# A row maximum in 22 loads, with parts of the late rows reduced over partitions by GpSimd

## The chip, the cores and the metric

The kernel runs on one core of a Trainium2 chip. The metric is the device time of one execution in microseconds, as the median of repeated runs. One further execution was recorded by the hardware profiler; every duration below comes from that record.

## The reference

The input `x` has the shape 32 x 512 x 1024 in float32. The output is the maximum over the last axis, 32 x 512 values:

```python
def reference(x):
    return np.max(x, axis=-1).astype(np.float32)
```

The first two axes are flattened, so there are 16,384 vectors of 1,024 values. In the kernel 128 of them lie across the 128 partitions. In this document a **row** is such a set: 128 partitions x 1,024 values, 512 KB. The whole input is 128 rows, and one output value per partition comes from each.

## The kernel before

`ring` is a buffer in SBUF with room for `RING = 45` rows. `BLOCKS` lists by hand how many rows each load brings: first 14, 13, 12 and so on, at the end single rows. The loop issues each load from SyncE's queue (line 57) into the next free stretch of the ring and, right after it, VectorE's `reduce_max` over the same stretch (line 58), which writes one column of `res` for each row. VectorE takes the loads in that order. A load into a stretch that VectorE has not yet reduced waits for it; the framework puts in these waits.

The last row comes in two halves of 512 values. The first goes to the ring (line 67) and the second to `tail` (line 68), whose element just ahead of the second half receives the maximum of the first (line 69), so that one reduce over 513 values gives the row's result (line 70). All loads use one queue; SyncE does nothing else. TensorE, ScalarE's compute and GpSimd are unused, but for four small constants that GpSimd writes at the start.

The output goes out in two stores from ScalarE's queue: the first block of 112 rows (line 73), which is held by hand behind the last reduce of the loop, and the second block of 16 rows at the very end (line 75).

Of the kernel before, what the change touches and what calls it, by code (L numbers as in the profile page):

```python
# [1 line left out]

# [4 lines left out]

F32 = mybir.dt.float32

BLOCKS = [
    [14, 13, 12, 11, 9, 8, 8, 7, 6, 5, 5, 4, 4, 3, 3],
    [2, 2, 2, 1, 1, 1, 1, 1, 1, 1, 1, 1],
]
RING = 45
SYNC = mybir.DependencyInfo(mybir.DependencyClass.Sync, mybir.DependencyReason.DATA)

@with_exitstack
def kernel(
    ctx: ExitStack,
    tc: tile.TileContext,
    x: bass.AP,
    out: bass.AP,
):
    nc = tc.nc
    P = 128
    X = mybir.AxisListType.X  # L30

    xf = x.flatten_outer_dims()
    N, D = xf.shape
    H = D // 2
    I = N // P
    of = out.flatten_outer_dims()

    once = ctx.enter_context(tc.tile_pool(name="once", bufs=1))
    ring = once.tile([P, RING, D], F32)
    res = once.tile([P, I], F32)  # L40

    PAD = 16
    tail = once.tile([P, PAD + H], F32)

    at = first = 0
    views = []
    for loads in BLOCKS:
        S = sum(loads) + (loads is BLOCKS[-1])
        xb = xf[first * P:(first + S) * P, :].rearrange("(p i) d -> p i d", p=P)
        dst = bass.AP(tensor=of.tensor, offset=of.offset + first * P, ap=[[S, P], [1, S]])  # L50
        views.append((dst, res[:, first:first + S]))
        b = 0
        for n in loads:
            if at + n > RING:
                at = 0
            xc = ring[:, at:at + n, :]
            nc.sync.dma_start(out=xc, in_=xb[:, b:b + n, :])  # L57
            reduce = nc.vector.reduce_max(out=res[:, first + b:first + b + n], in_=xc, axis=X)  # L58
            at += n
            b += n  # L60
        first += S
    assert first == I

    if at + 1 > RING:
        at = 0
    half = ring[:, at, :H]
    nc.sync.dma_start(out=half, in_=xb[:, b, :H])
    nc.sync.dma_start(out=tail[:, PAD:], in_=xb[:, b, H:])
    nc.vector.reduce_max(out=tail[:, PAD - 1:PAD], in_=half, axis=X)  # L69
    nc.vector.reduce_max(out=res[:, I - 1:], in_=tail[:, PAD - 1:], axis=X)  # L70

    store = nc.scalar.dma_start(out=views[0][0], in_=views[0][1])
    tc.add_manual_dep(store.ins, reduce.ins.name, SYNC, reason="behind the loads")
    nc.scalar.dma_start(out=views[1][0], in_=views[1][1])

# [1 line left out]
_INS = ['x']  # L79
_OUTS = [((32, 512), 'float32')]  # L80

# [23 lines left out]
```

## Time and profile before

| What | Value |
|---|---|
| Median of 10 runs | 164.97 us (164.91 to 165.22) |
| The profiled execution | 164.91 us, of which its span is 163.1 us |
| VectorE busy | 138.9 us, 29 reduces |
| VectorE idle before its reduces | 21.8 us, 20.1 of it before the first |
| Data moved | 67.11 MB of loads, in 29 loads; mean 412 GB/s over the span |
| First load (14 rows) reduced from | 20.13 us |
| Last reduce starts, lasts | 160.12 us, 0.69 us |

The span is the time from the first to the last instruction on the core; the other 1.8 us of the execution's own time lie around it. The share of the DMA engines in the table by slices can pass 1, since packets overlap a little. A wait is put down to the event that came last.

### The profile page before, as it was taken

Reading aid. Unit: us, or ns where it says so; the run is one execution under the profiler, and the core shown is the slowest. Engines: PE = TensorE matmul, PEld = TensorE weight load, DVE = VectorE, ACT = ScalarE, POOL = GpSimd, SP = SyncE. Lnnn points to the kernel's source line nnn. Section 1 sums busy time; section 2 is a strip of 40 time slices with the busy share of each in tenths; the row PEclk is TensorE's granted clock in tenths of the full one; section 3 lists DMA queues with packets and bytes.
Section 4 is the critical chain, followed back from the end, with each engine's and each line's share of the span. In section 5 each row is a group of like instructions: output and inputs, shape, how many; then the busy total and the mean of one; then the engine's idle time right before and its main releaser. Section 6 shows DMA issues by size and latency. Waiting matters only on the chain.

```text
span 163.1 us, 117 instructions
## 1 busy us (share of the span) xinstructions
DVE 138.9 (85%) x29; POOL 0.2 (0%) x4
## 2 busy tenths in 40 slices
DVE  0000099989998999999999999999999999999994
POOL 0000000000000000000000000000000000000000
DMA  6999999999989989999989999999999999999990
GB/s 225 450 450 450 434 418 418 418 402 554 410 386 420 464 387 433 434 434 434 466 386 450 434 450 410 410 445 412 432 423 434 422 422 420 424 411 409 411 369 16
DMA packets 4464, 67.18 MB, mean 412 GB/s; under 512 B 752, under 2 KB 752, under 8 KB 2160
## 3 DMA queue, kind: packets, MB, share of 16 engines
q1 hardware_dynamic: 4176, 67.11, 96.8%
q10 hardware_dynamic: 288, 0.07, 0.2%
HBM read 67.11 MB, written 0.07 MB: 412 GB/s over the span
## 4 chain that ended last, share of the span: by engine, by line
DVE 49%; DMA 48%; SPq 1%; issue 0%
DMA ring<-in_x_dram 48%; DVE res L58 48%; SPq L57 1%; DVE res L70 0%; DVE tail L69 0%
## 5 line engine op out<-in xcount | busy, mean ns | idle before, releaser
L58 DVE TENSOR_REDUCE res<-ring 128x1 f32<-128x1024 f32 (+12 forms) x27 | 137.6, 5162 | 21.8 <-DMA ring<-in_x_dram 21.8
L70 DVE TENSOR_REDUCE res<-tail 128x1 f32<-128x513 f32 x1 | 0.7, 687 | 0.0
L69 DVE TENSOR_REDUCE tail<-ring 128x1 f32<-128x512 f32 x1 | 0.7, 676 | 0.0
L90 POOL MEMSET const-bfloat16-1.0<- 128x1 bf16 x1 | 0.1, 103 | 0.0
L90 POOL MEMSET const-uint8-127<- 128x1 uint8 x1 | 0.1, 103 | 0.0
L90 POOL MEMSET const-float32-1.0<- 128x1 f32 x1 | 0.1, 100 | 0.0
L90 POOL MEMSET const-float32-0.0<- 128x1 f32 x1 | 0.1, 99 | 0.2 <-issue 0.2
## 6 DMA issues: line engine op xcount, KB each, us to landing
ring<-in_x_dram SPq DMA_DIRECT2D x2, 4096.0 KB, 25.6
ring<-in_x_dram SPq DMA_DIRECT2D x1, 7168.0 KB, 19.4
ring<-in_x_dram SPq DMA_DIRECT2D x1, 6656.0 KB, 34.7
ring<-in_x_dram SPq DMA_DIRECT2D x1, 6144.0 KB, 48.7
ring<-in_x_dram SPq DMA_DIRECT2D x1, 5632.0 KB, 28.4
ring<-in_x_dram SPq DMA_DIRECT2D x2, 2560.0 KB, 38.3
ring<-in_x_dram SPq DMA_DIRECT2D x1, 4608.0 KB, 24.7
ring<-in_x_dram SPq DMA_DIRECT2D x9, 512.0 KB, 13.8
```

The source lines that it names most:

```text
L57: nc.sync.dma_start(out=xc, in_=xb[:, b:b + n, :])
L58: reduce = nc.vector.reduce_max(out=res[:, first + b:first + b + n], in_=xc, axis=X)
L69: nc.vector.reduce_max(out=tail[:, PAD - 1:PAD], in_=half, axis=X)
L70: nc.vector.reduce_max(out=res[:, I - 1:], in_=tail[:, PAD - 1:], axis=X)
L90: nc = _bacc.Bacc("TRN2", target_bir_lowering=False, num_devices=1)
```

## The change

In the sequence of loads, `BLOCKS` becomes 18 loads with 126 rows, of 15, 15, 15, 8, 12, 11, 9, 8, 7, 7, 5 and 4, 3, 2, 2, 1, 1, 1 rows, numbered from 0; the last two rows come in halves, four more loads. The ring has 46 rows. SyncE's queue still issues all of them, now at line 181 (and 201 and 202 for the halves).

From six of the late loads a part of the last rows is taken from VectorE. `SHARED` names it: `9: (5, 2)` means that of load 9 the last 5 rows have their first 2 parts of 128 values each handled elsewhere. For such a part `turn` (line 131 on) has TensorE transpose each 128 x 128 piece into PSUM, ScalarE copy the result to SBUF (line 137), and GpSimd take its maximum over the partitions with `partition_all_reduce` (line 139), up to 1,024 columns in one instruction. `back` then has TensorE transpose row 0 of that result, 128 values at a time, into single columns of a small PSUM tile (line 157). VectorE reduces the rest of those rows into one more column of the same small tile (the second `maximum` in the loop), and later `merge` reduces over the columns of the tile into `res`. A load with more than 1,024 columns to turn is taken in two chunks, which is the case for load 9 alone: 1,024 and 256 columns.

The lists fix the order on each engine. `TENSOR` is the order of `turn` and `back`; `MERGE` says after which load's reduces which tile is merged; `in_turn` chains the instructions of an engine in the order in which the program records them. An item of `TENSOR` is recorded as soon as the loads that it needs have been issued in the program, and no more than three loads are issued ahead of the loop's position. Eight small VectorE instructions at the start build the identity matrix for the transposes.

```diff
--- before.py
+++ after.py
 BLOCKS = [
-    [14, 13, 12, 11, 9, 8, 8, 7, 6, 5, 5, 4, 4, 3, 3],
-    [2, 2, 2, 1, 1, 1, 1, 1, 1, 1, 1, 1],
+    [15, 15, 15, 8, 12, 11, 9, 8, 7, 7, 5],
+    [4, 3, 2, 2, 1, 1, 1],
 ]
-RING = 45
+RING = 46
+
+
+SHARED = {9: (5, 2), 11: (4, 2), 12: (2, 4), 14: (1, 2), 15: (1, 4), 17: (1, 2)}
+
+
+TENSOR = [
+    ("turn", 9, 0), ("turn", 9, 1), ("back", 9, 0), ("back", 9, 1),
+    ("turn", 11, 0), ("turn", 12, 0), ("back", 11, 0), ("turn", 14, 0),
+    ("turn", 15, 0), ("back", 12, 0), ("back", 14, 0), ("turn", 17, 0),
+    ("back", 15, 0), ("back", 17, 0),
+]
+
+MERGE = {10: (9,), 13: (11,), 16: (12,), 17: (14,), 20: (15, 17)}
...
     once = ctx.enter_context(tc.tile_pool(name="once", bufs=1))
+    turned = ctx.enter_context(tc.tile_pool(name="turned", bufs=2))
+    allr = ctx.enter_context(tc.tile_pool(name="allr", bufs=2))
+    psum = ctx.enter_context(tc.tile_pool(name="psum", bufs=2, space=bass.MemoryType.PSUM))
+    psmall = ctx.enter_context(tc.tile_pool(name="psmall", bufs=4, space=bass.MemoryType.PSUM))
     ring = once.tile([P, RING, D], F32)
     res = once.tile([P, I], F32)
 
     PAD = 16
-    tail = once.tile([P, PAD + H], F32)
-
-    at = first = 0
+    tails = once.tile([P, 2, PAD + H], F32)
+
+    latest = {}
+
+    def in_turn(engine, inst):
+
+        if engine in latest:
+            tc.add_manual_dep(inst.ins, latest[engine].ins.name, NOSYNC, reason="in turn")
+        latest[engine] = inst
+        return inst
+
...
+
+    ident = once.tile([P, P], F32)
+    colno = once.tile([P, P], F32)
+    rowno = once.tile([P, 32], F32)
+    in_turn("DVE", nc.vector.memset(ident, 1.0))
...
+    loads = []
+    first = at = 0
     views = []
-    for loads in BLOCKS:
-        S = sum(loads) + (loads is BLOCKS[-1])
+    for sizes in BLOCKS:
+        S = sum(sizes) + 2 * (sizes is BLOCKS[-1])
         xb = xf[first * P:(first + S) * P, :].rearrange("(p i) d -> p i d", p=P)
         dst = bass.AP(tensor=of.tensor, offset=of.offset + first * P, ap=[[S, P], [1, S]])
         views.append((dst, res[:, first:first + S]))
         b = 0
-        for n in loads:
+        for n in sizes:
             if at + n > RING:
                 at = 0
-            xc = ring[:, at:at + n, :]
-            nc.sync.dma_start(out=xc, in_=xb[:, b:b + n, :])
-            reduce = nc.vector.reduce_max(out=res[:, first + b:first + b + n], in_=xc, axis=X)
+            loads.append((at, n, xb[:, b:b + n, :], first + b))
             at += n
             b += n
         first += S
     assert first == I
 
-    if at + 1 > RING:
-        at = 0
-    half = ring[:, at, :H]
-    nc.sync.dma_start(out=half, in_=xb[:, b, :H])
-    nc.sync.dma_start(out=tail[:, PAD:], in_=xb[:, b, H:])
-    nc.vector.reduce_max(out=tail[:, PAD - 1:PAD], in_=half, axis=X)
-    nc.vector.reduce_max(out=res[:, I - 1:], in_=tail[:, PAD - 1:], axis=X)
+    def chunks(j):
+        m, parts = SHARED[j]
+        per = max(1, C // parts)
+        return [(r, min(per, m - r)) for r in range(0, m, per)]
+
+    def rows(j):
+        start, n, _, _ = loads[j]
+        return ring[:, start:start + n, :]
+
+    tops = {}
+    backs = {}
+
+    def turn(j, c):
+
+
+        m, parts = SHARED[j]
+        r, q = chunks(j)[c]
+        W = q * parts * P
+        ps = psum.tile([P, D], F32)
+        for i in range(q):
+            for c0 in range(parts):
+                k = i * parts + c0
+                in_turn("PE", nc.tensor.transpose(
+                    out=ps[:, k * P:(k + 1) * P],
+                    in_=rows(j)[:, loads[j][1] - m + r + i, c0 * P:(c0 + 1) * P],
+                    identity=ident,
+                ))
+        sb = turned.tile([P, D], F32)
+        in_turn("ACT", nc.scalar.copy(out=sb[:, :W], in_=ps[:, :W]))
+        top = allr.tile([P, D], F32)
+        in_turn("POOL", nc.gpsimd.partition_all_reduce(
+            top[:, :W], sb[:, :W], P, bass_isa.ReduceOp.max))
+        tops[j, c] = top
+
+    def share(j):
+        m, parts = SHARED[j]
+        if j not in backs:
+            fetched = psmall.tile([P, m, parts + (parts < C)], F32)
+            backs[j] = fetched
+        return backs[j]
+
+    def back(j, c):
+
+        m, parts = SHARED[j]
+        r, q = chunks(j)[c]
+        for i in range(q):
+            for c0 in range(parts):
+                k = i * parts + c0
+                in_turn("PE", nc.tensor.transpose(
+                    out=share(j)[:, r + i, c0:c0 + 1],
+                    in_=tops[j, c][0:1, k * P:(k + 1) * P],
+                    identity=ident[0:1, 0:1],
+                ))
+
+    def maximum(out, in_):
+        return in_turn("DVE", nc.vector.reduce_max(out=out, in_=in_, axis=X))
+
+    def merge(j):
+        for i in MERGE.get(j, ()):
+            _, k, _, c0 = loads[i]
+            q, _ = SHARED[i]
+            maximum(res[:, c0 + k - q:c0 + k], share(i))
+
+
+    issued = done = 0
+    todo = list(TENSOR)
+    for j in range(len(loads)):
+        while issued < len(loads) and issued < j + 3:
+            start, n, src, _ = loads[issued]
+            held = any(s < start + n and start < s + k for s, k, _, _ in loads[j:issued])
+            if held:
+                break
+            nc.sync.dma_start(out=rows(issued), in_=src)
+            issued += 1
+        while todo and (todo[0][0] == "back" or todo[0][1] < issued):
+            what, i, c = todo.pop(0)
+            (turn if what == "turn" else back)(i, c)
+        _, n, _, col = loads[j]
+        m, parts = SHARED.get(j, (0, 0))
+        if n > m:
+            maximum(res[:, col:col + n - m], rows(j)[:, :n - m, :])
+        if m and parts < C:
+            maximum(share(j)[:, :, parts], rows(j)[:, n - m:, parts * P:])
+        merge(j)
+    assert not todo
+
+    for t in range(2):
+        if at + 1 > RING:
+            at = 0
+        row = S - 2 + t
+        half = ring[:, at, :H]
+        at += 1
+        nc.sync.dma_start(out=half, in_=xb[:, row, :H])
+        nc.sync.dma_start(out=tails[:, t, PAD:], in_=xb[:, row, H:])
+        maximum(tails[:, t, PAD - 1:PAD], half)
+        merge(len(loads) + 2 * t)
+        last = maximum(res[:, I - 2 + t:I - 1 + t], tails[:, t, PAD - 1:])
+        merge(len(loads) + 2 * t + 1)
+        if t == 0:
+            latest_row = last
 
 
     store = nc.scalar.dma_start(out=views[0][0], in_=views[0][1])
-    tc.add_manual_dep(store.ins, reduce.ins.name, SYNC, reason="behind the loads")
```

In the list of instructions of the changed program, the order on VectorE from load 9 on is: 2 rows of load 9; the 5 x 768 part of load 9; 5 rows of load 10; merge of 9; the 4 x 768 part of load 11; 1 row and the 2 x 512 part of load 12; 2 rows of load 13; merge of 11; 1 row and the 1 x 768 part of load 14; the 1 x 512 part of load 15; load 16; merge of 12; the 1 x 768 part of load 17; merge of 14; the two halves of the one row; the first half of the other; merges of 15 and 17; the second half.

That list also has the waits that the framework put in. VectorE's reduces of the parts of loads 9, 11, 14, 15 and 17, which write into the small PSUM tile, each wait for TensorE's last `back` into the same tile. For load 12 it is the other way round: TensorE's `back` waits for VectorE's reduce.

## Prediction before the run

> **What bounds the kernel now.** The table of busy time first, then the chain that ended last, then the DMA issues.
>
> ```profile
> DVE 138.9 (85%) x29; POOL 0.2 (0%) x4
> DMA  6999999999989989999989999999999999999990
> ```
>
> VectorE (DVE) works 85% of the span. The second line, the DMA engines' busy share in 40 slices, is full from the second slice to the last but one: two resources are near their limit, and the end decides which one holds it.
>
> ```profile
> 1.62 48.73 DMA ring<-in_x_dram
> ...
> 63.72 30.29 DMA ring<-in_x_dram
> 94.01 0.02 issue
> 94.04 65.45 DVE res L58 x21
> 159.49 0.61 DVE tail L69
> 160.12 0.69 DVE res L70
> ```
>
> The columns are start, duration, what. Up to 94 us the transfers release VectorE each time; from there VectorE runs 65.45 us without a gap and sets the end. Those 21 reduces are 60 rows. A row costs 1.0667 us (the 14-row reduce takes 15,085 ns, the 13-row one 14,020; in between lie the starts of consecutive single rows, 1.126 us apart), so 60 x 1.0667 = 64.0, and 1.45 / 21 = 0.07 us is left for each instruction.
>
> ```profile
> ring<-in_x_dram SPq DMA_DIRECT2D x1, 256.0 KB, 9.6
> tail<-in_x_dram SPq DMA_DIRECT2D x1, 256.0 KB, 9.0
> 149.28 0.33 SPq L67 DMA_DIRECT2D ring<-in_x_dram  x1
> 150.52 0.33 SPq L68 DMA_DIRECT2D tail<-in_x_dram  x1
> ```
>
> The last half was issued at 150.52 and landed 9.0 us later, at 159.5. The reduce that needs it began at 160.12. So VectorE holds the end by only 0.6 us; behind it the transfers would. **That is all that a lighter VectorE can win at this end.** The arrival rate comes from VectorE's first waits, which a load ends: 14 rows at 20.13, 27 at 35.83, 39 at 50.37, thus 1.21 us a row.
>
> [...] VectorE's part and TensorE's `back` write different columns of one small tile and are ordered all the same. The trace before uses no PSUM and can't show it. [...]
>
> **The change, part by part.**
>
> *Loads.* Seven fewer. In the trace's packet records a packet of 57,344 B takes 2,116 ns and one of 4,096 B 162 ns: 27.2 B/ns and some 11 ns for each packet. Each engine carries eight packets of a load, so a load costs about 0.09 us, seven 0.6: the last landing moves from 159.5 to 158.9. Worth nothing, since VectorE ends later. Still, 15 rows first instead of 14 delay VectorE's start to 21.4, and loads 1 and 2 land 18.1 us apart where a 15-row reduce takes 16.1: idle 2.0 us twice. VectorE leaves load 2 at 21.4 + 3 x 16.07 + 4.0 = 73.7; loads 3 to 8, 55 rows, take 58.7 + 0.4, so it comes free at 132.8. Load 9 (rows 101 to 107) lands at 21.4 + 92 x 1.21 = 132.7. Its two full rows end at **135.0**.
>
> *SyncE.* The loads up to 8 wait for reduces long done before the queue runs dry (load 3 goes out at 37.5, with 45 rows queued until 57.6). From load 9 on, every load goes into a stretch whose last reader is at most load 6, done at 117. So no transfer is behind the tail's waits. The two stores come after VectorE as before; ScalarE's copies ahead of them in its queue end before VectorE does, or VectorE waits for them anyway.
>
> *Start.* Eight VectorE instructions for the identity[...] lie under the 21 us of the first load. VectorE's eight are under 3 us by the nearest row (676 ns for a 512-wide reduce). If one were uncovered: 0 to 3.
>
> *Added wait, the main term.* At 135.0 VectorE comes to the 5 x 768 part of load 9, which waits for TensorE's last `back` of load 9. No operation on that path is in the trace:
> [...]
>
> So VectorE stands from 135.0 to 142.2: **+7.2 us**. Everything after it on VectorE queues behind.
>
> *After it.* 5 x 768 values at 0.96 per ns take 4.06, load 10 takes 5.4, the merge 0.2: 151.9. The part of load 11 waits likewise: landed 143.7, [...] give 152.9: **+1.0**. TensorE does `turn` of load 12 (landed 147.3) ahead of that `back`, so even a free GpSimd gives about 151. The remaining 18 reduces hold 13,313 values: 13.9, plus 18 x 0.07 and 0.4 for merges that read what was just written: 15.5, to **168.4**. By the same prices the `back`s of 14, 15 and 17 come at 160.2, 162.8 and 163.6, VectorE at 162.0, 162.9 and 164.7: no further stall, by margins down to 0.1.
>
> *What it saves.* GpSimd takes 4,352 values of each partition, 4.5 us at 0.96 per ns. Longer first loads spend 3.6 on VectorE's start and idle (25.4 against 21.8); six parts and six merges in place of eleven smaller reduces about cancel. Without waits VectorE would end at 135.0 + 9.7 + 15.5 = 160.2, a mere 0.6 before 160.8; next in line would be the last landing, 158.9 and a half-row reduce of 0.7.
>
> Sum: 168.4 against 160.8 is **+7.6**: a span of 170.7, and 164.91 + 7.6 = 172.5 of its own time. The median before is 0.06 above the profiled execution: **172.6**.
>
> **Rivals.**
> - *GpSimd is the bound of the whole tail*, about 25 in 100. It gets 3,072 columns in five instructions after load 9, and its chunks of 11, 12 and 15 must pass one after another through the same waits. Repeating the schedule with 6 ns and 0.5 us an instruction gives 178, with 8 ns 183, with 10 ns 192[...]. For it: nothing here has timed this instruction. [...]
> - *The tail's helpers are quicker*, within the forecast: [...] the stalls at about 4 us in all: 168.6.
> - *The other side: VectorE never waits*, 3 in 100. The 4.5 us come off, end 160.2, time 164.4, faster by 0.4%. It decides at one place: the chain of load 9 must be back by about 135.3, since a stall above 0.3 us uses up what a measurement can tell, and 0.6 all of the gain. [...] the chain starts at 132.7. For it would speak a VectorE that is several us behind load 9's landing; by the waits above it is at most 0.1 behind.
> - *The change doesn't do what it says*: GpSimd takes the parts, but VectorE gets no freer, since it waits for each; that is the forecast itself. *No difference* (2 in 100) takes stalls of 0.3 to 0.9 us in all.
>
> **How the numbers follow.** A measurement of this kernel can tell about 0.2% from no change. Forecast 70 in 100, its own range 168.6 to 178; GpSimd-bound 25, of which I leave out what lies above 10 ns a column. Range **168.6 to 188**. Faster 0.03, same 0.02, slower 0.95.
>
> **What would show it.** In the changed profile VectorE should idle twice by 2 us before loads 1 and 2, then about 7 us before the first reduce into `fetched`, released by TensorE (TensorE by GpSimd); the DMA slices should fall silent near 159 while VectorE goes on to 168. GpSimd's instructions should be 4 to 5 us apart for 1,024 columns. It is wrong if that wait is under 1 us, if loads wait for ring space after 120 us, or if the last landing moves by over 1 us.

## The result, and the profile after

The changed kernel takes 170.81 us, the kernel before 164.96 in the same series: a ratio of 1.0351, with a 95% interval of 1.0342 to 1.036. It is slower by 5.85 us. The profiled execution's span is 168.9 us against 163.1.

The changed kernel's table of busy time, and from the table by slices VectorE (DVE), GpSimd (POOL) and the DMA engines:

```profile
PE 13.2 (8%) x68; PEld 10.5 (6%) x68; DVE 136.2 (81%) x39; ACT 5.9 (4%) x8; POOL 14.8 (9%) x11
...
DVE  3000099986999599999999999999999906979994
...
POOL 0000000000000000000000000000000082197510
DMA  6999997999999699898999899898999999999400
```

VectorE works 2.7 us less than before, and yet the kernel ends later. Two places show it. In the last fifth VectorE's row has a hole (a 0 and a 6) just where GpSimd's row begins; and the DMA row falls silent two slices before the end, where before it was full to the last slice but one. The transfers no longer stand close behind VectorE: something holds VectorE back. In the timeline:

```profile
149.96 0.33 SPq L202 DMA_DIRECT2D tails<-in_x_dram  x1
...
165.91 0.68 DVE L164 TENSOR_REDUCE res<-tails 128x1 f32<-128x513 f32 x1
```

The last half is issued at 149.96, half a microsecond earlier than before (150.52), and its reduce starts at 165.91, where it was 160.12.

The table of waits of the changed kernel, VectorE's two large rows (columns: total, times, longest):

```profile
DVE res L164 <- DMA ring<-in_x_dram: 22.8, 3, 18.8
...
DVE fetched L164 <- PE fetched L157: 6.7, 2, 5.6
```

The first row is the start: 18.8 us for load 0, and 2 us each for loads 1 and 2. The second is new: VectorE stood 6.7 us, in two waits, for TensorE's `back` (line 157), before a reduce into the small PSUM tile `fetched`. The timeline gives the way that led to both (start, duration, engine; in brackets the idle time before, and who ended it). Shown are VectorE's lines and those of the two relays, a **relay** being the way of a load's parts through TensorE, ScalarE, GpSimd and back through TensorE; other work in between is left out:

```profile
132.86 2.37 PE L131 MATMUL ps<-ident,ring 128*128 128x128 f32 x10 [132.86 <-DVE res L164]
134.84 1.29 ACT L137 COPY sb<-ps 128x1024 f32<-128x1024 f32 x2 [132.84 <-PE ps L131]
135.94 4.27 POOL L139 PARTITION_ALL_REDUCE top<-sb  x2 [135.51 <-ACT sb L137]
139.22 1.42 PE L157 MATMUL fetched<-ident,top 1*128 1x1 f32 x10 [3.99 <-POOL top L139]
140.68 4.16 DVE L164 TENSOR_REDUCE fetched<-ring 128x5 f32<-128x3840 f32 x1 [5.59 <-PE fetched L157]
143.90 1.94 PE L131 MATMUL ps<-ident,ring 128*128 128x128 f32 x8 [3.26 <-DMA ring<-in_x_dram]
144.75 5.48 DVE L164 TENSOR_REDUCE res<-ring 128x5 f32<-128x5120 f32 x1
145.94 1.01 ACT L137 COPY sb<-ps 128x1024 f32<-128x1024 f32 x1 [9.82 <-PE ps L131]
147.05 3.22 POOL L139 PARTITION_ALL_REDUCE top<-sb  x1 [6.83 <-ACT sb L137]
150.14 0.16 DVE L164 TENSOR_REDUCE res<-fetched 128x5 f32<-128x15 f32 x1
150.32 1.01 PE L157 MATMUL fetched<-ident,top 1*128 1x1 f32 x8 [0.83 <-POOL top L139]
151.37 3.36 DVE L164 TENSOR_REDUCE fetched<-ring 128x4 f32<-128x3072 f32 x1 [1.07 <-PE fetched L157]
```

The relay of load 9 runs from 132.86 to the last `back` at 140.64. VectorE, ready at 135.09 and with its data landed at 132.77, waits 5.59 us for it. The relay of load 11 starts when that load lands and ends at 151.33; VectorE, done with the merge of load 9 at 150.30, waits another 1.07 us. The chain that ended last names the second relay and not the first:

```profile
...
107.92 35.85 DMA ring<-in_x_dram
143.77 0.14 issue
143.90 1.96 PE ps L131 x8
...
145.94 1.02 ACT sb L137
146.96 0.08 issue
147.05 3.23 POOL top L139
150.28 0.04 issue
150.32 1.02 PE fetched L157 x8
151.35 0.02 issue
151.37 3.36 DVE fetched L164
...
```

Read backward: VectorE's part of load 11, the `back`s, GpSimd, ScalarE, the transposes, the landing. Load 9 and its wait of 5.59 us are not on it. This will matter below.

### The profile page after: what moved, and what is told of

It is laid out like the page before. It is cut to its first block, busy times and chain, and to the rows that moved or that the text cites. A ratio compares the mean times of both kernels' runs of the same rounds, so it can differ in the third digit from the quotient of the medians.

```text
span 168.9 us, 290 instructions
## 1 busy us (share of the span) xinstructions
PE 13.2 (8%) x68; PEld 10.5 (6%) x68; DVE 136.2 (81%) x39; ACT 5.9 (4%) x8; POOL 14.8 (9%) x11
## 4 chain that ended last, share of the span: by engine, by line
DVE 46%; DMA 44%; POOL 2%; PE 2%; issue 1%; another core or an unknown queue 1%; SPq 1%; ACT 1%; DVEq 0%; ACTq 0%
DMA ring<-in_x_dram 44%; DVE res L164 42%; DVE fetched L164 4%; POOL top L139 2%; PE ps L131 1%; DVE tails L164 1%; SPq L181 1%; PE fetched L157 1%; ACT sb L137 1%; DVEq L239 0%; ACTq L137 0%
## 5 line engine op out<-in xcount | busy, mean ns | idle before, releaser
L164 DVE TENSOR_REDUCE res<-ring 128x15 f32<-128x15360 f32 (+8 forms) x15 | 121.2, 8111 | 22.8 <-DMA ring<-in_x_dram 22.8
L139 POOL PARTITION_ALL_REDUCE top<-sb x7 | 14.6, 2126 | 146.1 <-ACT sb L137 142.8
L131 PE MATMUL ps<-ident,ring 128*128 128x128 f32 x34 | 8.7, 425 | 139.7 <-DVE res L164 132.9
L164 DVE TENSOR_REDUCE fetched<-ring 128x1 f32<-128x768 f32 (+4 forms) x6 | 11.2, 1888 | 6.7 <-PE fetched L157 6.7
L131 PEld LDWEIGHTS ps<-ident,ring 128*128 128x128 f32 x34 | 6.4, 220 | 140.5 <-DVE res L164 132.8
L137 ACT COPY sb<-ps 128x1024 f32<-128x1024 f32 (+2 forms) x7 | 4.6, 678 | 152.8 <-PE ps L131 151.4
L157 PE MATMUL fetched<-ident,top 1*128 1x1 f32 x34 | 4.5, 243 | 8.7 <-POOL top L139 6.5
L157 PEld LDWEIGHTS fetched<-ident,top 1*128 1x128 f32 x34 | 4.1, 212 | 10.4 <-POOL top L139 7.8
L164 DVE TENSOR_REDUCE res<-tails 128x1 f32<-128x513 f32 x2 | 1.4, 682 | 0.0
L164 DVE TENSOR_REDUCE tails<-ring 128x1 f32<-128x512 f32 x2 | 1.4, 676 | 0.0
## 6 DMA issues: line engine op xcount, KB each, us to landing
ring<-in_x_dram SPq DMA_DIRECT2D x1, 5632.0 KB, 21.4
```

What stands on the lines that cost most here:

```text
L131: in_turn("PE", nc.tensor.transpose(out=ps[:, k * P:(k + 1) * P], in_=rows(j)[:, loads[j][1] - m + r + i, c0 * P:(c0 + 1) * P], identity=i ...
L137: in_turn("ACT", nc.scalar.copy(out=sb[:, :W], in_=ps[:, :W]))
L139: in_turn("POOL", nc.gpsimd.partition_all_reduce(top[:, :W], sb[:, :W], P, bass_isa.ReduceOp.max))
L157: in_turn("PE", nc.tensor.transpose(out=share(j)[:, r + i, c0:c0 + 1], in_=tops[j, c][0:1, k * P:(k + 1) * P], identity=ident[0:1, 0:1],))
L164: return in_turn("DVE", nc.vector.reduce_max(out=out, in_=in_, axis=X))
```

## The experiments

The theory to be tested: VectorE waits because its part of a shared row and TensorE's `back` write into one small PSUM tile, and the `back` was recorded first; the last relay that VectorE waits for, load 11's, sets the end. Its rivals: the loads themselves are the loss; VectorE is slowed by the other engines' traffic; GpSimd is just too slow, so that the wait would move to the merges; or each wait costs its own length.

Each time stands against the kernel before in the same series, 164.97 us for the first four and 165.00 for the others.

**The loads alone** (`e1_loads_only`).

```diff
-SHARED = {9: (5, 2), 11: (4, 2), 12: (2, 4), 14: (1, 2), 15: (1, 4), 17: (1, 2)}
+SHARED = {}
-TENSOR = [
...
-]
+TENSOR = []
-MERGE = {10: (9,), 13: (11,), 16: (12,), 17: (14,), 20: (15, 17)}
+MERGE = {}
```

> The changed kernel's 22 loads with nothing shared: VectorE reduces every row whole. Theory (VectorE is held by waits for TensorE in the tail; the loads alone cost a later start and two idle spells of 2 us): VectorE free at 132.8, then 7 + 19 rows less the two halved ones, 24 x 1.0667 + 9 x 0.07 = 26.2, and 2.7 for the four halves: 132.8 + 2.2 ... in sum VectorE's end near 163.9 against 160.8 before, so 168.0 us. Rival A (the loads alone make the whole loss, sharing costs nothing): 170.8. Rival B (the loads cost nothing, all the loss is the sharing): 165.

Measured: 167.87 us, ratio 1.0177 (1.0161 to 1.0192). The 22 loads with nothing shared lose 2.9 us by themselves; half of the 5.85 us is theirs, and the sharing adds the other half. In the timeline VectorE runs without a gap from load 2 on to its last reduce at 163.11, which lasts 0.69.

**The backs recorded later** (`e2_backs_later`). Every engine has the same work in the same order; only the moment at which a `back` is recorded moves behind VectorE's part of the same load.

```diff
-        while todo and (todo[0][0] == "back" or todo[0][1] < issued):
+        while todo and todo[0][1] < (j if todo[0][0] == "back" else issued):
...
         merge(j)
-    assert not todo
+    for what, i, c in todo:
+        (turn if what == "turn" else back)(i, c)
```

> The same work, but each back of a load is recorded after VectorE's part of that load, so TensorE waits for VectorE and not the other way round. Theory: the waits of 5.6 and 1.1 us at the parts of loads 9 and 11 vanish, the merges come late enough to find their tiles ready, VectorE ends near 160.3 and the time is 164.5, at most 165.5. Rival A (GpSimd's chain is late for the merges too, so that the wait only moves): 166 to 169. Rival B (VectorE is slowed by TensorE's and GpSimd's traffic, not by waits): 170 or more.

Measured: 164.27 us, ratio 0.9959 (0.9947 to 0.9972), faster than the kernel before by 0.7 us, a small difference but clear of the noise. Its timeline for VectorE and GpSimd around loads 9 to 11:

```profile
135.00 4.15 DVE L164 TENSOR_REDUCE fetched<-ring 128x5 f32<-128x3840 f32 x1
135.95 4.27 POOL L139 PARTITION_ALL_REDUCE top<-sb  x2 [135.52 <-ACT sb L137]
139.06 5.48 DVE L164 TENSOR_REDUCE res<-ring 128x5 f32<-128x5120 f32 x1
144.46 0.17 DVE L164 TENSOR_REDUCE res<-fetched 128x5 f32<-128x15 f32 x1
144.54 3.35 DVE L164 TENSOR_REDUCE fetched<-ring 128x4 f32<-128x3072 f32 x1
```

GpSimd starts at the same instant as in the changed kernel (135.95, 135.94) and takes as long. VectorE no longer waits for it: it does its part at 135.00 and load 10 at 139.06, and when it comes to the merge at 144.46, the `back`s are long in. So GpSimd's speed alone was not at fault, nor the other engines' traffic, since both are unchanged. Its table of waits has no row of VectorE for TensorE at all. Load 12 had this order in the changed kernel already: there TensorE waits 2.2 us for VectorE, and VectorE's part starts at 155.77 without a wait. One changed condition is worth 6.5 us.

**A tile of VectorE's own** (`e3_own_tile`). The order of recording stays as in the changed kernel; VectorE's part goes to SBUF.

```diff
+    mine = once.tile([P, len(loads), 8], F32)
...
+    def parts_of(j):
+        return SHARED[j][1]
...
-            maximum(res[:, c0 + k - q:c0 + k], share(i))
+            top = share(i)[:, :, parts_of(i)]
+            maximum(top, share(i)[:, :, :parts_of(i)])
+            in_turn("DVE", nc.vector.tensor_tensor(
+                out=res[:, c0 + k - q:c0 + k], in0=top, in1=mine[:, i, :q], op=ALU.max))
...
-            maximum(share(j)[:, :, parts], rows(j)[:, n - m:, parts * P:])
+            maximum(mine[:, j, :m], rows(j)[:, n - m:, parts * P:])
```

> The order of recording stays as changed, but VectorE writes its part of a shared row into a tile of its own in SBUF; a merge is then a reduce over TensorE's columns and a maximum of two operands, six small instructions more. Theory (the wait comes from sharing one small PSUM tile with TensorE): waits at the parts vanish, VectorE ends near 161.3, 165.5 us. Rival (the wait comes from the order on the engines, whichever tile is written): unchanged, 170.8 to 172.

Measured: 165.11 us, ratio 1.0007 (0.9999 to 1.0016). The part of load 9 starts at 135.21 with no wait ahead of it. TensorE's order is that of the changed kernel, so the wait came from the shared tile. Whether a tile of VectorE's own in PSUM would do as well as this one in SBUF was not tried. Against the second experiment it costs 0.84 us, for six small instructions on VectorE that each begin some 0.2 us after the one they read from; with them the whole gain is gone.

**Load 9 not shared** (`e4_no9`). This takes away the longest wait, and tells waits that add up from relays that overlap.

```diff
-SHARED = {9: (5, 2), 11: (4, 2), 12: (2, 4), 14: (1, 2), 15: (1, 4), 17: (1, 2)}
+SHARED = {11: (4, 2), 12: (2, 4), 14: (1, 2), 15: (1, 4), 17: (1, 2)}
...
-    ("turn", 9, 0), ("turn", 9, 1), ("back", 9, 0), ("back", 9, 1),
...
-MERGE = {10: (9,), 13: (11,), 16: (12,), 17: (14,), 20: (15, 17)}
+MERGE = {13: (11,), 16: (12,), 17: (14,), 20: (15, 17)}
```

> Load 9 is taken out of the sharing, VectorE reduces its 7 rows whole: the wait of 5.6 us goes. Theory (load 11's way through TensorE, ScalarE and GpSimd, which starts when load 11 lands at 143.8, releases VectorE at 151.4 whatever came before): VectorE comes to the part of load 11 at about 146 and waits there 5.4 us, so that the time stays at 170.8, within 0.4. Rival (the waits add up, each is worth its length): 5.6 less and 1.1 more work, 166.3.

Measured: 170.82 us, ratio 1.0354 (1.034 to 1.0368): no change at all from the changed kernel. Its timeline, in which VectorE reduces loads 6 to 10 whole from 107.06 on:

```profile
107.06 38.84 DVE L163 TENSOR_REDUCE res<-ring 128x9 f32<-128x9216 f32 x5
...
150.47 1.01 PE L156 MATMUL fetched<-ident,top 1*128 1x1 f32 x8 [0.89 <-POOL top L138]
...
151.52 3.36 DVE L163 TENSOR_REDUCE fetched<-ring 128x4 f32<-128x3072 f32 x1 [5.62 <-PE fetched L156]
```

VectorE is through with load 10 at 145.90, more than four microseconds sooner than before. The wait of 5.6 us is gone from load 9 and stands, equally long, at load 11, whose part starts at 151.52 where it started at 151.37 before. That is what the chain had said.

**GpSimd's work doubled, once for load 9 and once for load 11** (`e5_gpsimd9_twice`, `e6_gpsimd11_twice`). The all-reduce of 1,024 columns is issued twice in a row, for one load; the diff is that of load 9, the other kernel has (11, 0) in its place.

```diff
-        in_turn("POOL", nc.gpsimd.partition_all_reduce(
-            top[:, :W], sb[:, :W], P, bass_isa.ReduceOp.max))
+        for _ in range(2 if (j, c) == (9, 0) else 1):
+            in_turn("POOL", nc.gpsimd.partition_all_reduce(
+                top[:, :W], sb[:, :W], P, bass_isa.ReduceOp.max))
```

> The changed kernel with GpSimd's 1,024-column all-reduce of load 9 done twice, 3.1 us more on that chain. Theory (load 11's chain releases VectorE at 151.4 and swallows what is ready before): the wait at load 9 grows from 5.6 to 8.7, the wait of 1.07 at load 11 goes, so 3.1 - 1.1 = 2.0 us more: 172.9. Rival (load 9's wait sets the end by itself): 3.1 more, 173.9. Rival (GpSimd's time is hidden): 170.8.

> The changed kernel with GpSimd's all-reduce of load 11 done twice. Theory: load 11's chain sets VectorE's end, so all of the 3.1 us show: 173.9. Rival (load 9's wait is the one that counts, load 11's has slack): 171 to 172.

Measured: 172.93 us with load 9's doubled, 174.01 with load 11's, thus +2.1 and +3.2 on the changed kernel's 170.81. One GpSimd instruction more costs 3.3 us on VectorE's wait either way. In the first kernel the wait of load 9 is 8.91 us in place of 5.59, and the part of load 11 then starts with no wait left:

```profile
144.06 4.16 DVE L165 TENSOR_REDUCE fetched<-ring 128x5 f32<-128x3840 f32 x1 [8.91 <-PE fetched L158]
...
153.60 3.35 DVE L165 TENSOR_REDUCE fetched<-ring 128x4 f32<-128x3072 f32 x1
```

In the second it is the wait of load 11 that takes all of it, 4.37 us in place of 1.07:

```profile
140.71 4.16 DVE L165 TENSOR_REDUCE fetched<-ring 128x5 f32<-128x3840 f32 x1 [5.59 <-PE fetched L158]
...
154.71 3.36 DVE L165 TENSOR_REDUCE fetched<-ring 128x4 f32<-128x3072 f32 x1 [4.37 <-PE fetched L158]
```

Load 9's relay had 1.07 us of slack against load 11's. Load 11's had none.

**Neither load 9 nor load 11 shared** (`e8_no9_no11`), the same edit as for load 9, done for both.

> The changed kernel without the sharing of loads 9 and 11. Theory: no wait of several us is left, but the parts of loads 14 and 15 still wait for TensorE, some 0.5 and 1.2 us, since their chain starts only as those loads land: VectorE ends near 163.9, 168.2 us, no better than with nothing shared (167.87). Rival (the waits for loads 9 and 11 were the whole trouble, the rest of the sharing pays): loads alone less the 1,024 + 256 + 512 + 256 = 2,048 values taken off, 2.1 us, plus 0.6 for merges: 166.4.

Measured: 168.12 us, ratio 1.0186 (1.0172 to 1.02), against 167.87 and 1.0177 (1.0161 to 1.0192) with nothing shared: what is left of the sharing wins nothing. Its row in the table of waits:

```profile
DVE fetched L163 <- PE fetched L156: 1.8, 2, 1.4
```

The parts of loads 14 and 15 now wait, 0.41 and 1.42 us. That is 1.8 of the 2.1 us which the remaining sharing takes off VectorE; the merges, 0.6 us by the estimate made beforehand, are more than the rest.

**A quicker start on top of the better version** (`e7_shorter_first`).

```diff
-    [15, 15, 15, 8, 12, 11, 9, 8, 7, 7, 5],
+    [14, 14, 13, 11, 12, 11, 9, 8, 8, 7, 5],
```

> The version with the backs recorded later, with loads of 14, 14, 13, 11, 12, 11, 9, 8, 8, 7, 5 rows in the first block (the same 107 rows by load 9), so that VectorE idles some 23 us in place of 25.4. Theory: VectorE then keeps up with the transfers to the end, and the last landing at 158.9 and a half-row reduce hold it: end 159.6 to 159.8, 163.8 us. Rival (VectorE's end is set by the merges and GpSimd's chain, not by its own backlog): unchanged, 164.3.

Measured: 164.29 us, ratio 0.9953 (0.994 to 0.9967). The expected half microsecond did not come, and the rival's number did, though not its reason: VectorE has no wait for TensorE in this run's table. The expectation rested on less idle time of VectorE, and that is what failed. Its waits for loads, in this run and then in the version with 15 rows first:

```profile
DVE res L164 <- DMA ring<-in_x_dram: 22.9, 6, 17.8
...
DVE res L164 <- DMA ring<-in_x_dram: 22.8, 3, 18.8
```

The first wait is 1.0 us shorter, but there are six in place of three, and the sum is the same. The last of the six is for load 8:

```profile
124.51 10.88 DVE L164 TENSOR_REDUCE res<-ring 128x8 f32<-128x8192 f32 x2 [0.21 <-DMA ring<-in_x_dram]
...
135.31 4.15 DVE L164 TENSOR_REDUCE fetched<-ring 128x5 f32<-128x3840 f32 x1
```

VectorE was done with 92 rows at 124.31. The version with 15 rows first was done with 93 at 125.30, about the time of one row later, so nothing of the earlier start was left. VectorE comes to the part of load 9 at 135.31 here, at 135.00 there, and after that both versions have the same work on VectorE, some 25 us, and nearly no gaps. I had counted the earlier start and too little of the waits that come back when VectorE catches up with the transfers sooner. Whether still smaller loads ahead of load 9 would win the half microsecond was not tried.

## Why the prediction was right

It said 172.6 us, and 170.81 was measured, by the mechanism that it named: VectorE waits for TensorE's `back`s. Step by step:

- *The start.* Forecast: VectorE starts at 21.4, idles 2.0 us twice, is free at 132.8 and done with two rows of load 9 at 135.0. Measured: 21.30, 1.99 and 1.98, 132.82, 135.09. The identity cost nothing visible: VectorE's eight small instructions end at 2.51, and its first reduce starts 18.79 us later, when load 0 has landed. Some slips of the working carry no weight: the sum for the end of load 2 is 73.6 and not 73.7 (measured 73.73), and up to 94 us the transfers release VectorE for five of the first seven loads of the kernel before, not each time.
- *Loads and SyncE.* No load waited for ring space in the tail, and by the trace's landing records the last half landed at 158.9, as forecast. It brought nothing, since VectorE ended at 166.59.
- *The wait at load 9.* Forecast 7.2 us, measured 5.59. This is the mis-sized term of the sum. What the steps of a relay take was the author's estimate; no trace had shown one of them. Measured, TensorE's transposes into one tile start 0.21 us apart, ScalarE's copy of 1,024 columns took 1.01 us, and GpSimd, from 135.94 on, took 3.22 us for 1,024 columns and 1.14 for 256, together 4.27 for the 1,280, or 3.3 ns a column. The last `back` ended at 140.64, where the forecast had VectorE released at 142.2. The sign that GpSimd's instructions for 1,024 columns would be 4 to 5 us apart, estimated likewise, did not come true: those of loads 11 and 12 start 3.6 us apart (147.05 and 150.69). That the sum came so near is partly luck.
- *The wait at load 11.* Forecast 1.0, measured 1.07. Both its ends came about 1.6 us earlier, VectorE at 150.30 (151.9 forecast) and the release at 151.37 (152.9), each because a relay came home sooner than estimated. Their difference therefore hardly depends on what the steps of a relay take.
- *The remaining 18 reduces.* Forecast 15.5 us, measured 15.22 (151.37 to 166.59), without a wait of note.
- *Without waits*, the forecast had VectorE end at 160.2. The second experiment ended at 160.12 (159.43 + 0.69).

What the prediction had wrong is the standing of its two waits. It added +7.2 and +1.0, and called the first the main term. The sum was right, but the fourth experiment shows that taking away the first moves the end by nothing. The relay of load 11 starts at its landing and would have released VectorE at about 151.4 in any case; the wait at load 9 only decided where VectorE stood until then. So the 1.8 us by which the forecast was too high belong to load 11's relay, which came home 1.5 us sooner, and to the reduces after it, 0.3 us; the 1.6 us at load 9 are not among them. The prediction came near it when it wrote that even a free GpSimd gives about 151 at load 11, and did not draw the conclusion.

The rival of a GpSimd that bounds the whole tail fell: with 14.6 us of all-reduces in 25 us, it idles between them. The first all-reduce took as long as the later ones of its size (3,224 ns each). The other side, where VectorE never waits, is real and lies where it was put, at 164.4 (164.27 measured), but needs the order of recording changed. No run showed that VectorE's part has to come after the `back`s: with the opposite order VectorE's table of waits has none for TensorE, and a wait would be TensorE's. In the second experiment's trace even that one does not show: TensorE's waits before the `back`s, 6.2 us in four, are put down to GpSimd.

## What to carry to other kernels

Where two engines wrote into one tile, the framework ordered them here as they were recorded, though they touch different columns (VectorE waited 5.59 us at load 9, and not at all with the `back`s recorded later); look in the list of instructions for which of them waits, and record the busy engine's write first, so that the engine with time to spare does the waiting. Before you count a wait as a gain, see whether the chain that ended last goes through it: VectorE's longest wait in the tail, 5.6 us, was worth nothing by itself, and the relay behind the wait of 1.07 us held the end. In this kernel, work handed to a long relay paid only where the bound engine had other work until it returned: against the same loads with nothing shared, the sharing cost 2.9 us when VectorE's parts had to wait for the relay, and won 3.6 when only the merges needed it.

## What the runs showed of the hardware

GpSimd's `partition_all_reduce` with max over 128 partitions of float32 took 3,224 ns for 1,024 columns, 1,784 for 512 and 1,142 for 256 by the profile, about 2.7 ns a column and 0.45 us besides; one more of 1,024 columns lengthened VectorE's wait by 3.32 us at load 9 and 3.30 at load 11. ScalarE's copies out of PSUM took 1,012 ns for 1,024 columns, 586 for 512 and 374 for 256. A VectorE reduce that writes its five results to PSUM took as long (4.16 us) as one that writes them to SBUF (4.14 us in the third experiment), and GpSimd at work beside it made no difference to it that can be seen: 4.16 us after GpSimd had finished in the changed kernel, 4.15 beside it in the second experiment.
